# A planned matmul-tanh-multiply kernel: fewer split multiplications on VectorE, and the general path's transfers on GpSimd's queue

## The chip, the core and the metric

One core of a Trainium2 chip. The metric is the device time of one execution in microseconds (us), the median of the runs of a kernel; less is better. Engines are named as in the profile: PE is TensorE, DVE is VectorE, ACT is ScalarE, POOL is GpSimd, SP is SyncE. A "q" behind an engine (SPq, POOLq) is its instruction sequencer, which issues DMAs and handles waits.

## The reference, cut

```python
x  : (16, 512, 1024) float32      # 8192 rows of 1024
w1 : (1024, 768), w2 : (1024, 768) float32
y1 = matmul(x, w1); y2 = matmul(x, w2)
return tanh(y1) * y2              # (16, 512, 768) float32
```

Two matrix products with the same left side, and one element-wise combination of both.

## The kernel before, in words

**Tiling.** The 8192 rows are 64 row tiles of 128 (`mt` 0 to 63). The 768 columns of an output are cut in a first 512 (`F`) and a last 256 (`G`). The weights lie in SBUF as float16 in three column blocks of 512: `a` is w1's first 512, `b` is w2's first 512, `g` holds w1's last 256 beside w2's last 256. The inner dimension of 1024 is cut in two halves of four 128-deep slices (`KH` = 4).

**Head and triples.** The first four row tiles (`HEAD`) are computed plainly (lines 419 to 434) while the weights still arrive. The other 60 are taken in 20 triples (i = 0 to 19) of three row tiles. Three row tiles by two halves by three column blocks would be 18 block products; each triple gets by with 15 (`p0` to `p14`, line 441), by sums of left blocks (`A_SUMS`, operations `S...`, line 410, on DVE) and of weight blocks (`B_SUMS`, once for all triples), and by sums of results (`C_OPS`). A product is four matmuls of 128x128 by 128x512 that accumulate in one PSUM bank. Eight banks rotate.

**What happens to the results.** `C_OPS` lists the operations of a triple behind the products, and what each needs:
- `copyN`, `seedN` (line 446, ACT): copy a bank to SBUF (`arena`), or into another bank on which a later product goes on accumulating (`seed16` before `p2`; `seed56` before `p8`).
- `addN` (line 449, DVE): the sum of a bank and a copy, back into a bank or into SBUF. `p9` waits for `add312`, `p12` for `add64`, `p4` for `add60`, `p3` and `p2` for `add52` and `seed16`, and `p14` overwrites what `seed56` reads.
- `t0`, `t1`, `t2` (line 455, ACT): tanh of 512 columns into the output tile `o`; `th0` to `th2` the same for the last 256.
- `m0`, `m1`, `m2` (line 459, `c_mul`, DVE): multiply the tanh in `o` with the 512 columns of y2 in a bank, in place; `mh0` to `mh2` the same for the last 256. With this the bank is free for a later product, and the row tile can be stored (line 416, SP's queue).

A name with a number behind a dot is that operation in that triple: `m1.10` is `m1` of triple 10. Products of the next triple are mixed in (`PE_ORDER`, line 69): `p4.10` runs between products of triple 11.

**Where a multiplication is split.** Lines 704 to 711 enter the multiplications. For `m0`, `m1`, `m2` of every triple but the last they make two operations of 256 columns (`m0x` and `m0y`), each with a cost of 0.335 for the planner; for the last triple one of 512 columns at 0.6.

**What sets the order.** The class `Planner` (lines 75 to 223) plays the whole kernel through at build time from these costs, due times and needs: at each step it takes the operation that can start soonest, by due time among those that tie, and gives each accumulation chain one of the eight banks. The products' order on PE is fixed (`plan.strict`, line 502); that of DVE, ACT and of the queues comes from the planner, and is then kept in the program (`pin`). So a cost that is entered differently can change the order of neighbouring operations and the numbers of the banks.

**The flag and the general path.** The fast way holds for inputs whose absolute sums lie in certain limits. ACT sums them on the way (lines 379 to 387), DVE and PE make one flag of them near the end (`f1` to `f5`), and all five engines read it (line 766) and branch (line 767). If the flag is set, `general_path` (line 771) computes everything again in a plain loop. For the inputs used here the flag is zero and its body is not executed; a short block for the other side of the branch evens out the semaphores.

Of the kernel before, what the change touches and what calls it, by code (L numbers as in the profile page):

```python
# [226 lines left out]
def kernel(  # L227
# [7 lines left out]
    nc = tc.nc  # L235
# [9 lines left out]
    TRIPLES = (MT - HEAD) // 3  # L245
# [4 lines left out]
    WARM = 512, 512, 512, 512, 512, 512, 512  # L250
    FILL = 512, 512, 256
    AHEAD, FREE = 4, 3
    S_AHEAD = 4.0
    LATER = {mt: 66.0 + 13.0 * mt for mt in range(HEAD - 1)}
    bf16, f16, f32, i32 = mybir.dt.bfloat16, mybir.dt.float16, mybir.dt.float32, mybir.dt.int32

    xf = x.flatten_outer_dims().rearrange("(mt p) k -> mt p k", p=P)
    of = out.flatten_outer_dims().rearrange("(mt p) n -> mt p n", p=P)
    wr = [w.rearrange("(ko ki) n -> ki ko n", ki=P) for w in (w1, w2)]
# [403 lines left out]
    def needed(i, v):  # L663
        return min([slot_of[i, o[0]] for o in C_OPS if o[1] == "p" and o[4] == v] + [needed(i, u) - 0.5 for u, a, b, _ in A_SUMS if v in (a, b)])

    for i in range(TRIPLES):
        for name, kind, needs, *_ in C_OPS:
            soonest[i, name] = max([until[i, n] for n in needs] + ([slot_of[i, name]] if kind == "p" else []))
            until[i, name] = soonest[i, name] + TIME[kind] + 0.2
        for v, a, b, how in A_SUMS:  # L670
            op(f"S{v}.{i}", {"dve": 0.335}, None, x_needs(i, a) + x_needs(i, b), x_sum, i, v, a, b, how,
               hold=needed(i, v) - S_AHEAD if i > 1 else 0.0,
               behind=[f"{r}.{i - S_BUFS}" for r in a_readers[v]] if i >= S_BUFS else first_done)
            for u in (a, b):
                if not u & (u - 1):
                    xt_readers[HEAD + 3 * i + (u.bit_length() - 1) // 2].append(f"S{v}.{i}")
        for o in C_OPS:
            name, kind, needs = o[:3]
            needs = [f"{n}.{i}" for n in needs]
            chains = sorted({(i, p) for p in o[3:6] if isinstance(p, str) and p[0] == "c"})  # L680
            if kind == "p":
                needs += x_needs(i, o[4]) + w_needs(o[5])
                op(f"{name}.{i}", {"pe": SLOT}, slot_of[i, name], needs, product, i, *o[3:], chains=chains,
                   behind=[f"m{HEAD - 1}y0{KO - 1}"] if (name, i) == ("p3", TRIPLES - 1) else [])
                if not o[4] & (o[4] - 1):
                    xt_readers[HEAD + 3 * i + (o[4].bit_length() - 1) // 2].append(f"{name}.{i}")
                continue
            if kind in ("seed", "copy", "add"):
                before = []
                if o[3][0] == "s":  # L690
                    before = [f"{r}.{i - C_BUFS}" for r in readers[o[3]]] if i >= C_BUFS else all_casts
                if kind == "add":
                    op(f"{name}.{i}", {"dve": 0.6}, None, needs, c_add, i, *o[3:], behind=before, chains=chains, seeds=True)
                else:
                    op(f"{name}.{i}", {"act": 0.495}, None, needs, c_copy, i, *o[3:], behind=before, chains=chains, seeds=True)
                continue
            r = o[3]
            mt = HEAD + 3 * i + r
            due = soonest[i, name] + LAST
            if kind in ("t", "th"):  # L700
                lo, n = (0, F) if kind == "t" else (F, G)
                op(f"{name}.{i}", {"act": 0.5 if n == F else 0.285}, due, needs, c_tanh, i, r, o[4], lo, n, o[5],
                   behind=reuse_out(mt) + ([f"{FIRST_READER[name]}.{i}"] if i == TRIPLES - 1 and name in FIRST_READER else []), chains=chains)
            elif kind == "m" and i < TRIPLES - 1:
                for t in range(2):
                    op(f"{name}{'xy'[t]}.{i}", {"dve": 0.335}, due + 1, needs, c_mul, i, r, o[4], t * G, G, t * G, chains=chains)
                    outs[mt].append(f"{name}{'xy'[t]}.{i}")
            else:
                lo, n, at = (0, F, 0) if kind == "m" else (F, G, G)
                op(f"{name}.{i}", {"dve": 0.6 if n == F else 0.335}, due + 1, needs, c_mul, i, r, o[4], lo, n, at, chains=chains)  # L710
                outs[mt].insert(0 if kind == "m" else 1, f"{name}.{i}")
    for mt in range(MT):
        i = (mt - HEAD) // 3 if mt >= HEAD else -1
# [23 lines left out]
    for mt in range(HEAD, MT):  # L737
        i, r = divmod(mt - HEAD, 3)
# [16 lines left out]
    for n in sorted(soon, key=lambda n: plan.start_of[n]):  # L755
        o = plan.ops[n]
# [3 lines left out]
    for n in order:  # L760
        if n not in soon:
            o = plan.ops[n]
# [8 lines left out]
def general_path(tc, xf, wr, of, N, F):  # L771
    nc = tc.nc
    P = 128
    MT, _, K = xf.shape
    KO = K // P
    G = N - F
    f16, f32, i32 = mybir.dt.float16, mybir.dt.float32, mybir.dt.int32
    with ExitStack() as stack:
        pool = lambda name, bufs, **k: stack.enter_context(tc.tile_pool(name=name, bufs=bufs, **k))
        once = pool("general", 1)  # L780
        work = pool("general_work", 2)
        ps = pool("general_ps", 2, space=bass.MemoryType.PSUM)

        def powers(total, n, tag):
            p = work.tile([P, n], f32, name=tag)
            nc.vector.tensor_scalar(p.bitcast(i32), total.bitcast(i32), 0x7F800000, None, ALU.bitwise_and)
            nc.vector.tensor_scalar(p, p, 2.0 ** -100, 2.0 ** 100, ALU.max, ALU.min)
            r = work.tile([P, n], f32, name=tag + "r")
            nc.vector.reciprocal(r, p)
            return p, r  # L790

        ones = once.tile([P, P], f32, name="g_ones")
        nc.vector.memset(ones, 2.0 ** -12)
        asum = once.tile([P, 2, KO], f32, name="g_asum")
        junk = once.tile([P, K], f16, name="g_junk")
        wf = [once.tile([P, KO, N], f32, name=f"g_wf{t}") for t in range(2)]
        wh = [once.tile([P, KO, N], f16, name=f"g_wh{t}") for t in range(2)]
        w_p = once.tile([P, 2], f32, name="g_wp")
        for t in range(2):
            nc.sync.dma_start(wf[t], wr[t])  # L800
            for k in range(KO):
                nc.scalar.activation(junk[:, :N], wf[t][:, k, :], ACT.Abs, accum_out=asum[:, t, k:k + 1])
            part = work.tile([P, 1], f32, name="g_part")
            nc.vector.tensor_reduce(part, asum[:, t, :], mybir.AxisListType.X, ALU.add)
            total = ps.tile([P, F], f32, name="g_total")
            nc.tensor.matmul(total[:, :1], ones, part, start=True, stop=True)
            p, r = powers(total[:, :1], 1, "g_w")
            nc.vector.tensor_copy(w_p[:, t:t + 1], p)
            for k in range(KO):
                nc.vector.tensor_scalar(wh[t][:, k, :], wf[t][:, k, :], r, None, ALU.mult)  # L810

        with tc.For_i(0, MT, 1) as i:
            xt32 = work.tile([P, K], f32, name="g_x")
            nc.sync.dma_start(xt32, xf[i])
            s = work.tile([P, 1], f32, name="g_s")
            nc.scalar.activation(junk, xt32, ACT.Abs, scale=2.0 ** -12, accum_out=s)
            p, r = powers(s, 1, "g_xp")
            xh = work.tile([P, K], f16, name="g_xh")
            nc.vector.tensor_scalar(xh, xt32, r, None, ALU.mult)
            xt = work.tile([P, KO, P], f16, name="g_xt")  # L820
            nc.sync.dma_start_transpose(xt, xh)
            scale = work.tile([P, 2], f32, name="g_scale")
            nc.vector.tensor_scalar(scale, w_p, p, None, ALU.mult)
            o = work.tile([P, N], f32, name="g_o")
            for lo, n in ((0, F), (F, G)):
                y = [ps.tile([P, F], f32, name=f"g_y{t}") for t in range(2)]
                for t in range(2):
                    for k in range(KO):
                        nc.tensor.matmul(y[t][:, :n], xt[:, k, :], wh[t][:, k, lo:lo + n],
                                         start=k == 0, stop=k == KO - 1)  # L830
                nc.scalar.activation(o[:, lo:lo + n], y[0][:, :n], ACT.Tanh, scale=scale[:, :1])
                nc.vector.scalar_tensor_tensor(o[:, lo:lo + n], y[1][:, :n], scale[:, 1:2], o[:, lo:lo + n],
                                               ALU.mult, ALU.mult)
            nc.sync.dma_start(of[i], o)


# [28 lines left out]
```

## Time and profile before

| | |
|---|---|
| median of 3 runs (lowest, highest) | 298.52 us (298.41, 298.60) |
| the profiled execution | 298.88 us |
| its span, first to last instruction | 297.1 us, so 1.8 us lie around it |
| PE busy | 290.1 us (98%), granted clock 0.998 |
| DVE busy | 259.7 us (87%), 597 instructions |
| ACT busy | 226.3 us (76%) |
| POOL busy | 50.4 us (17%) |

The profile is one execution. A row of the groups of instructions gives line, engine, operation, what is written from what, the count, then busy time and the mean of one, then the engine's idle time ahead of them and what ended it. A row of the timeline gives the start and the length in us, and stands for several instructions where it ends with x2 or more. Records of one engine overlap a little, since an instruction's last part lies beside the next one's first: the distance from start to start is what one costs its engine. On PE a 512-column matmul is recorded with 379 ns, and in a full stretch one starts every 0.216 us.

### The profile page before, as it was taken

The numbers are of one execution on the slowest core, as the hardware profiler recorded it, in microseconds if no ns is written. First come the engines' busy times: TensorE is split into PE (matmuls) and PEld (weight loads), VectorE is DVE, ScalarE is ACT, GpSimd is POOL, SyncE is SP. The second block draws the span as 40 slices with busy tenths as digits, with TensorE's granted clock in tenths as the row PEclk, the third lists the DMA queues.
The fourth block names the chain that finished last, engine by engine and source line by source line (L and its number), as shares of the span: only waits on it lengthen the run. The fifth ranks groups of instructions, "written<-read, shape, count | busy, mean of one in ns | idle before, by whom it ended". The sixth has DMA issues, their size and how long they took to land. (4 is left out here: it accounts for less than half of the span.)

```text
span 297.1 us, 4747 instructions
## 1 busy us (share of the span) xinstructions
PE 290.1 (98%) x1374; PEld 132.4 (45%) x1374; DVE 259.7 (87%) x597; ACT 226.3 (76%) x453; POOL 50.4 (17%) x129
## 2 busy tenths in 40 slices
PE   8999999999999999999999999999999999999993
PEld 3445444444444444444444444444444444444441
DVE  1679899989999998989989899898989989898884
ACT  2596898799978979798797988768677776868441
POOL 0073133132221111213111111202021110000000
PEclk9999999999999999999999999999999999999999
DMA  6999999999999999999999999999999999041234
GB/s 230 387 300 207 182 157 147 189 202 260 197 251 250 225 294 274 162 177 286 221 204 192 285 240 206 282 158 308 151 269 198 279 253 282 18 162 53 107 143 161
DMA packets 84428, 63.51 MB, mean 214 GB/s; under 512 B 62768, under 2 KB 66608, under 8 KB 84400
## 3 DMA queue, kind: packets, MB, share of 16 engines
q1 hardware_dynamic: 73600, 44.84, 63.7%
q0 software_dynamic: 9792, 16.78, 34.9%
q10 hardware_dynamic: 1008, 1.57, 1.5%
q8 instruction: 11, 0.18, 0.3%
q14 instruction: 17, 0.14, 0.2%
HBM read 39.85 MB, written 25.17 MB: 219 GB/s over the span
## 5 line engine op out<-in xcount | busy, mean ns | idle before, releaser
L443 PE MATMUL bank<-b,early_x 128*128 128x512 f16 x640 | 148.4, 379 | 0.1
L443 PEld LDWEIGHTS <-early_x 128*128 128x128 f16 x800 | 78.0, 98 | 94.7 <-DVE early_x L411 0.6
L453 DVE TENSOR_TENSOR bank<-bank,arena 128x512 f32<-128x512 f32 x100 | 69.6, 697 | 13.1 <-ACT arena L447 8.9
L447 ACT ACTIVATE arena<-bank 128x512 f32<-128x512 f32 x100 | 59.3, 596 | 28.5 <-PE bank L443 28.3
L461 DVE TENSOR_TENSOR o<-o,bank 128x256 f32<-128x256 f32 (+1 forms) x177 | 68.1, 420 | 6.5 <-ACT o L456 5.7
L380 ACT ACTIVATE junk<-xh 128x1024 f16<-128x1024 f16 x60 | 63.4, 1056 | 0.2
L443 PEld LDWEIGHTS <-xT 128*128 128x128 f16 x400 | 39.0, 98 | 47.5 <-issue 1.3
L443 PE MATMUL bank<-b,xT 128*128 128x512 f16 x240 | 58.3, 379 | 0.0
L456 ACT ACTIVATE o<-bank 128x256 f32<-128x256 f32 (+1 forms) x80 | 34.4, 436 | 16.1 <-DVE bank L453 12.8
L443 PE MATMUL bank<-wh,xT 128*128 128x512 f16 x160 | 41.1, 379 | 0.4 <-DVE bank L453 0.4
L443 PE MATMUL bank<-wh,early_x 128*128 128x512 f16 x160 | 40.9, 379 | 0.0
L352 POOL DMA_DIRECT2D xh<-in_x_dram x60 | 31.7, 529 | 35.8 <-ACT o L456 20.2
L480 POOL CAST held<-xT 128x1 f32<-128x1 f16 x54 | 13.6, 252 | 137.8 <-DMA xT<-xh 137.7
L411 DVE TENSOR_TENSOR early_x<-early_x,xT 128x512 f16<-128x512 f16 x80 | 33.3, 419 | 0.5
L447 ACT ACTIVATE bank<-bank 128x512 f32<-128x512 f32 x40 | 21.6, 578 | 8.8 <-DVE bank L453 7.7
L456 ACT ACTIVATE o<-arena 128x512 f32<-128x512 f32 x40 | 25.2, 629 | 0.6 <-DVE arena L453 0.5
L420 PE MATMUL bank<-wh,xT 128*128 128x512 f16 x72 | 18.5, 379 | 0.4 <-DVE wh L358 0.3
L411 DVE TENSOR_TENSOR early_x<-xT,xT 128x512 f16<-128x512 f16 x40 | 16.8, 420 | 0.0
L411 DVE TENSOR_TENSOR early_x<-xT,early_x 128x512 f16<-128x512 f16 x40 | 16.8, 419 | 0.0
L453 DVE TENSOR_TENSOR bank<-arena,bank 128x512 f32<-128x512 f32 x20 | 13.9, 695 | 1.5
L453 DVE TENSOR_TENSOR arena<-arena,bank 128x512 f32<-128x512 f32 x20 | 13.6, 682 | 0.0
L453 DVE TENSOR_TENSOR arena<-bank,arena 128x512 f32<-128x512 f32 x20 | 13.6, 681 | 0.0
(47 smaller groups left out, 136.3 us busy)
## 6 DMA issues: line engine op xcount, KB each, us to landing
out_dram<-o SPq DMA_DIRECT2D x60, 384.0 KB, 5.5
xh<-in_x_dram POOLq DMA_DIRECT2D x60, 256.0 KB, 6.4
arena<-in_w_dram SPq DMA_DIRECT2D x12, 256.0 KB, 5.4
early_x<-in_x_dram SPq DMA_DIRECT2D x8, 256.0 KB, 5.0
arena<-in_w_dram ACTq DMA_DIRECT2D x4, 256.0 KB, 5.8
wh<-in_w_dram POOLq DMA_DIRECT2D x8, 128.0 KB, 5.2
xT<-xh SPq DMA_TRANSPOSE x57, 6.6
out_dram<-o SPq DMA_DIRECT2D x4, 128.0 KB, 2.4
```

The source lines that it names most:

```text
L352: pin(nc.gpsimd.dma_start(xh(mt), xf[mt]))
L380: pin(nc.scalar.activation(junk[:, :src.shape[-1]], src, ACT.Abs, scale=scale, accum_out=sums[:, column:column + 1]))
L411: pin(engine[e].tensor_tensor(x_operand(i, v), x_operand(i, a), x_operand(i, b), OP[how]))
L420: pin(nc.tensor.matmul(bank(chain)[:, :rhs.shape[-1]], xt(mt)[:, k, :], rhs, start=first, stop=k == KO - 1, skip_group_check=True))
L443: pin(nc.tensor.matmul(place(i, dst), x_operand(i, a)[:, k, :], w_rhs(b, k), start=begins and k == 0, stop=k == KH - 1, skip_group_check=T ...
L447: pin(nc.scalar.activation(place(i, dst), place(i, src), ACT.Copy, scale=float(sign)))
L453: pin(nc.vector.tensor_tensor(place(i, dst), a, b, ALU.add if signs == (1, 1) else ALU.subtract))
L456: pin(nc.scalar.activation(out_tile(HEAD + 3 * i + r)[:, lo:lo + n], place(i, src)[:, :n], ACT.Tanh, scale=float(sign)))
L461: pin(nc.vector.tensor_tensor(o, o, place(i, src)[:, at:at + n], ALU.mult))
L480: pin(nc.gpsimd.tensor_copy(held, xt(mt)[:, 0, :1]))
```

## The change

Two edits. A new constant `HALVED = 4` takes the place of `TRIPLES - 1` in the condition that splits a multiplication: `m0`, `m1`, `m2` are now split in triples 0 to 3 alone, and are one operation of 512 columns in triples 4 to 19 (before, in triple 19). And in `general_path` the loads of the weights and of the row tiles, and the store of the result, are issued from GpSimd's queue instead of SyncE's; its transpose stays on SyncE.

```diff
-    S_AHEAD = 4.0
+    S_AHEAD, HALVED = 4.0, 4
...
-            elif kind == "m" and i < TRIPLES - 1:
+            elif kind == "m" and i < HALVED:
                 for t in range(2):
                     op(f"{name}{'xy'[t]}.{i}", {"dve": 0.335}, due + 1, needs, c_mul, i, r, o[4], t * G, G, t * G, chains=chains)
...
         for t in range(2):
-            nc.sync.dma_start(wf[t], wr[t])
+            nc.gpsimd.dma_start(wf[t], wr[t])
...
             xt32 = work.tile([P, K], f32, name="g_x")
-            nc.sync.dma_start(xt32, xf[i])
+            nc.gpsimd.dma_start(xt32, xf[i])
...
-            nc.sync.dma_start(of[i], o)
+            nc.gpsimd.dma_start(of[i], o)
```

## The prediction

> **What bounds the kernel now.** I asked first whether PE ever waits where the change acts, which is from triple 4 on, from about 88 us. The busy times of all engines in that stretch (columns: length, then busy us and instructions of PE, PEld, DVE, ACT, POOL, granted clock, DMA share, GB/s):
>
> ```profile
> 85.00:270.00 185.00, 185.00 (x859) 83.86 (x858) 168.42 (x387) 148.51 (x300) 28.41 (x76) 1.00 1.07 221
> ```
>
> PE is busy for 185.00 of 185.00 us at the full clock, and 185 us by 859 matmuls is 0.215 us each, the same as their distance from start to start. So this is not slow matmuls under a full label: PE is at its rate. The waits of PE over the whole run, in full:
>
> ```profile
> PE bank L330 <- DVE ones L752: 1.1, 1, 1.1
> PE bank L443 <- DVE bank L453: 0.4, 1, 0.4
> PE bank L420 <- DVE wh L358: 0.3, 1, 0.3
> PE bank L370 <- DMA early_x<-in_x_dram: 0.3, 1, 0.3
> ```
>
> Three of the four lie in the first 14 us. The one at line 443 is at 51.86 us, in the triples that stay split. DVE is busy for 91% of the stretch and still makes PE wait for nothing, so DVE time saved there is no kernel time in itself.
>
> **Part 1, the whole multiplications.** 15 triples (4 to 18) by 3 lose a pair of halves and gain one whole: 90 instructions out, 45 in. Their rows, by shape:
>
> ```profile
> L461 DVE TENSOR_TENSOR o<-o,bank 128x256 f32<-128x256 f32 x174 | 66.2, 415 | 5.6 <-ACT o L456 5.1
> ...
> L461 DVE TENSOR_TENSOR o<-o,bank 128x512 f32<-128x512 f32 x3 | 2.1, 685 | 0.9 <-ACT o L456 0.7 <-issue 0.2
> ```
>
> The means alone give 2 x 415 - 685 = 145 ns a pair, but records overlap. What a half costs DVE is its distance to the next, and the timeline of DVE in triple 10 shows it:
>
> ```profile
> 171.69 0.41 DVE L461 TENSOR_TENSOR o<-o,bank 128x256 f32<-128x256 f32 x1
> 172.18 0.70 DVE L453 TENSOR_TENSOR bank<-bank,arena 128x512 f32<-128x512 f32 x1
> 172.79 1.07 DVE L461 TENSOR_TENSOR o<-o,bank 128x256 f32<-128x256 f32 x3
> 173.78 0.68 DVE L453 TENSOR_TENSOR arena<-arena,bank 128x512 f32<-128x512 f32 x1
> 174.38 0.42 DVE L411 TENSOR_TENSOR early_x<-xT,xT 128x512 f16<-128x512 f16 x1
> 174.84 0.70 DVE L453 TENSOR_TENSOR bank<-bank,arena 128x512 f32<-128x512 f32 x1
> 175.45 0.68 DVE L453 TENSOR_TENSOR arena<-bank,arena 128x512 f32<-128x512 f32 x1
> ```
>
> Three halves from 172.79 to 173.78 are 0.33 us each; a 512-column operation takes 0.60 (173.78 to 174.38). A pair costs 0.66 and a whole 0.60: 0.06 x 45 = 2.7 us of DVE time, 0.18 of each triple's 12.95, all of it beside a full PE. As PE has no gap there to give back, I count 0.
>
> Can it cost? A whole one can't be interrupted for 0.60 instead of 0.33 us, so what is urgent behind it comes up to 0.27 later, and the planner reorders around it. The built program's order shows what moves: SP's and POOL's queues keep theirs; on DVE, `add8` goes ahead of `add52` in triples 4, 7 and 10; on ACT, at the same places, `seed16` goes behind `t1` and the next triple's `seed56`; bank numbers are renamed. With triple 10's rows in the new order: `m0.10` from 171.69 to a next start at 172.29, `add312.11` there (0.11 later), `m2.10` 172.89, `add64.11` 173.49 (0.29 earlier), `add8.10` 174.55 (behind the copy that ends at 174.51), `add52.10` 175.15, ending 175.85. On ACT, `t1.10` at 175.27, `seed56.11` 175.77, `seed16.10` 176.27 to 176.85. Who waits for that:
>
> ```profile
> 175.57 1.07 ACT L447 ACTIVATE bank<-bank 128x512 f32<-128x512 f32 x2 [0.45 <-DVE bank L453]
> ```
>
> ```profile
> 177.16 1.03 PE L443 MATMUL bank<-wh,early_x 128*128 128x512 f16 x4
> 178.03 1.24 PE L443 MATMUL bank<-b,xT 128*128 128x512 f16 x5
> ```
>
> The two seeds end at 176.16 and 176.65. `p14.11` (177.16) has 0.51 to spare behind `seed56` now, and 0.81 in the new order (end 176.35); `p3.10` (178.03) has 1.87 behind `seed16` now and 1.18 then. `p9` starts 1.42 us or more behind `add312` in triples 4 to 18, so 0.11 to 0.2 more is covered.
>
> The shortest cover is that of the multiplication itself: `p7` two triples on takes the bank that `m1` frees.
>
> ```profile
> 180.14 1.08 DVE L461 TENSOR_TENSOR o<-o,bank 128x256 f32<-128x256 f32 x3
> ...
> 181.48 0.81 PE L443 MATMUL bank<-wh,xT 128*128 128x512 f16 x3
> ```
>
> The row at 180.14 is `mh1.10`, `m1x.10`, `m1y.10`; the last ends at 181.22, 0.27 ahead of PE, and so it is, within 0.02, in ten of the 13 triples from 4 to 16 (0.60 in the others). One whole multiplication from 180.47 ends at 181.16: 0.06 earlier, not later. `p3.18` at 280.79 has 0.26 behind `seed16.18`, whose order stays.
>
> **The last triple** has no cover left, and small things count. PE's gaps there are 0.06 us at 285.27, 0.06 at 286.63 and 0.14 at 289.70, 0.26 in all (a 256-column matmul starts 0.109 before the next):
>
> ```profile
> 285.27 1.02 PE L443 MATMUL bank<-b,early_x 128*128 128x512 f16 x4
> ...
> 289.70 1.89 PE L443 MATMUL bank<-b,xT 128*128 128x512 f16 x8
> ```
>
> In the built order the filler matmuls of line 420 that stood before `p5.19` and `p4.19` move behind `p14.19`, and `add60.19` goes ahead of `mh0.18`. `m1.18` spares 0.06, so `add2.19` ends at 285.16 and `p5.19` starts at 285.21 (0.11 idle behind `p0.19`). `th0.18` at 284.44 and `copy56.19` at 284.73 let `add60.19` run 285.36 to 286.06, `p4.19` 286.11. Two more products of 0.86 and eight fillers of 0.109 bring `p3.19` to 289.57; the chain behind `p4` (3.07 us from 286.63 to 289.70 now) would allow 289.18. So `p3.19` starts 0.13 earlier, and what follows it is unchanged: -0.13 us. The bounds here are -0.54 (all 0.26 of gaps, and the 0.28 by which DVE's last multiplication waits for its engine behind the last matmul) and +0.27 (one blocking that nothing covers). I take -0.13.
>
> **Part 2, GpSimd's queue.** `general_path` doesn't run, so its transfers cost nothing by either queue. What does run is the other side of the branch, which evens semaphores: SP has one bump instead of five, POOL two waits and one software-queue bump. POOL reads the flag at 275.5 and then idles to the final barrier at 296.3, 20 us of cover. The same kind of bump took 0.03 us at the start; the dearest POOL row, the L352 transfers, is 0.53 each. SP's four bumps fewer are 0.3 us, but SP then waits for the last store to land:
>
> ```profile
> SPq L860 <- DMA out_dram<-o: 0.2, 1, 0.2
> ```
>
> The wait only grows. With the cover gone on either side, it would be 0.3 less, or 0.5 more (SP's time from its branch, 294.7, to its first wait behind it, 295.2, in the trace); I count 0, since both covers are long.
>
> **The sum.** 298.88 - 0.13 = 298.75 for the profiled execution, which lies 0.36 over the median; so 298.4 for the median.
>
> **The rivals.**
> - **PE starts to wait for whole multiplications** (slower). The place is `p7` behind `m1`. It decides from 0.27 us: a whole `m1` that starts more than 0.32 later than `m1x` does now makes PE wait (0.27, and the 0.06 by which it ends sooner). For it speaks that DVE is 91% busy and that its order is fixed in advance; against it that nothing ahead of `m1` changes and that it ends 0.06 sooner. If a 0.60 block too many stood ahead in those ten triples, (0.60 - 0.33) x 10 = 2.7, 301.1 us; in three of them, the reordered ones, 0.8, 299.2. Chance 0.08. The Trainium skill (Perfetto Trace Analysis, Optimizing Scalar/DVE Operations) has the rule that speaks against this change: where VectorE isn't saturated but causes bubbles elsewhere, smaller instructions let work finish sooner. By that rule undoing the split would bring bubbles; the trace has no bubble in 85 to 270 us for the split to have healed, so it doesn't bear the rule out here.
> - **The tail gives all it has** (faster): -0.54, 298.0; still within 0.2%. A gain above that would need PE to run faster than 0.216 us a matmul, or the wait at 51.86 us to go, and the order is the same up to there. Chance of that 0.04.
> - **The branch side costs**: +0.5, 298.9, if POOL or SP became last; against it the 20 us. Within 0.2% too.
> - That only the multiplications change anything (the general path's edit does nothing here) is part of the forecast.
>
> **How the numbers follow.** About 0.2% (0.6 us) is what a measurement of this kernel can tell from no change. No change that can be told: 0.87, with the branch side and the full tail in it. Slower by PE's waits: 0.08, and 0.01 for what I don't see: 0.09. Faster: 0.04. The range is 298.0 (the whole tail) to 298.9 (a branch cost, or one uncovered block with the median's own spread), and leaves out under 0.2.
>
> **What would show it.** PE busy for the whole of 85 to 270 again; 84 halves and 48 wholes at line 461; DVE's busy share lower with PE's the same; `p3.19` at 289.6; SP's wait for the last store longer than 0.2. PE waits on line 461 or 453 between 88 and 270 us would prove me wrong.

## The result, and the profile after

The changed kernel takes 298.24 us, the median of 22 runs (297.88 to 298.70). 22 runs of the kernel before beside it have a median of 298.70 us, so the three runs known beforehand were some 0.2 us low. The ratio is 0.9982 [0.9975, 0.9989]: about 0.5 us less, just under the bound of 0.2%. The forecast was 0.13 us. The profiled execution took 298.26 us with a span of 296.7 (before: 298.88 and 297.1).

From triple 4 on PE has no gap, as before, and DVE is busy for 2.2 us less. The busy times from 85 to 270 us of the kernel after (columns as before):

```profile
85.00:270.00 185.00, 185.00 (x859) 83.87 (x857) 166.20 (x346) 148.20 (x300) 28.51 (x76) 1.00 1.11 220
```

The waits of PE over its whole run, in full. None lies behind 52 us:

```profile
PE bank L330 <- DVE ones L752: 1.3, 1, 1.3
PE bank L370 <- DMA early_x<-in_x_dram: 0.4, 1, 0.4
PE bank L443 <- DVE bank L453: 0.3, 1, 0.3
PE bank L420 <- ACT xT L356: 0.2, 1, 0.2
```

The multiplications by shape (count, then busy us and mean ns of one), 84 halves and 48 wholes:

```profile
L461 DVE TENSOR_TENSOR o<-o,bank 128x256 f32<-128x256 f32 x84 | 33.5, 418 | 5.6 <-ACT o L456 5.2
L461 DVE TENSOR_TENSOR o<-o,bank 128x512 f32<-128x512 f32 x48 | 31.8, 681 | 0.6 <-ACT o L456 0.3 <-DMA out_dram<-o 0.2
```

Triple 10 on DVE; the kernel runs 0.10 later here, because it starts 0.23 later in its span and has not made up all of that:

```profile
171.79 0.68 DVE L461 TENSOR_TENSOR o<-o,bank 128x512 f32<-128x512 f32 x1
172.39 0.69 DVE L453 TENSOR_TENSOR bank<-bank,arena 128x512 f32<-128x512 f32 x1
172.99 0.68 DVE L461 TENSOR_TENSOR o<-o,bank 128x512 f32<-128x512 f32 x1
173.58 0.68 DVE L453 TENSOR_TENSOR arena<-arena,bank 128x512 f32<-128x512 f32 x1
174.18 0.42 DVE L411 TENSOR_TENSOR early_x<-xT,xT 128x512 f16<-128x512 f16 x1
174.64 0.69 DVE L453 TENSOR_TENSOR arena<-bank,arena 128x512 f32<-128x512 f32 x1
175.25 0.69 DVE L453 TENSOR_TENSOR bank<-bank,arena 128x512 f32<-128x512 f32 x1
```

`m0.10`, `add312.11`, `m2.10` and `add64.11` follow each other at 0.60, and `add8.10` (174.64) now stands ahead of `add52.10` (175.25), as the built order said. ACT and PE behind them:

```profile
175.90 1.06 ACT L447 ACTIVATE bank<-bank 128x512 f32<-128x512 f32 x2
```

```profile
177.26 1.03 PE L443 MATMUL bank<-wh,early_x 128*128 128x512 f16 x4
178.13 0.59 PE L443 MATMUL bank<-b,xT 128*128 128x512 f16 x2
```

In the first row `seed56.11` ends at 176.48 and `seed16.10` at 176.96, so `p14.11` (177.26) has 0.78 to spare and `p3.10` (178.13) has 1.17.

The last triple on PE:

```profile
284.34 1.03 PE L443 MATMUL bank<-b,xT 128*128 128x512 f16 x4
285.31 1.94 PE L443 MATMUL bank<-b,early_x 128*128 128x512 f16 x8
287.09 1.89 PE L443 MATMUL bank<-wh,early_x 128*128 128x512 f16 x8
288.82 1.04 PE L420 MATMUL bank<-wh,xT_kept 128*128 128x256 f16 x8
289.69 1.89 PE L443 MATMUL bank<-b,xT 128*128 128x512 f16 x8
```

From `p0.19` (284.34) to `p3.19` (289.69) it takes 5.35 us; before, 5.46 (284.24 to 289.70). This is the 0.11 us that the change gains on PE. In the profile it only cancels the 0.10 that the head was late: the last store is issued at 293.38 us in both. Yet the span ends 0.38 us sooner. **What the two executions differ by lies behind the last store.** There the sequencer of SP waits for the stores, and the landing of the last one is faster. The first fence of each pair is of before, the second of after; first the page's row of instruction packets (packets, MB, share), then the last store alone (count, size, us from issue to landing), then SP's wait for stores at line 860 (us, times, longest):

```profile
q14 instruction: 17, 0.14, 0.2%
```

```profile
q14 instruction: 16, 0.13, 0.1%
```

```profile
out_dram<-o SPq DMA_DIRECT2D x1, 128.0 KB, 2.6
```

```profile
out_dram<-o SPq DMA_DIRECT2D x1, 128.0 KB, 2.3
```

```profile
SPq L860 <- DMA out_dram<-o: 0.7, 2, 0.4
```

(Before: 0.2.) The trace has the single events. A store is done when 16 increments of its semaphore are there, each sent by a packet of 4 bytes. Before, 15 of the last store's arrive from 295.41 to 295.58 us, and the sixteenth at 296.02. After, all arrive from 295.41 to 295.64. Before, the last of these 4-byte packets begins at 295.359 us, and 6 ns later an 8 KB instruction packet of 309 ns. The trace does not say which DMA engine moves a packet; that both are on one engine is read from these 6 ns. And before, DVE's jump over the code of `general_path` to the kernel's last block takes 0.57 us (branch at 293.49, first instruction behind it at 294.06); after, 0.21. The 309 ns packet and the long jump are present in one kernel and absent from the other. The packet begins 1.87 us behind the branch. DVE is already past the jump then, by 1.30 us, so it does not wait for this packet.

**Theory.** The end is the later of two things, and about 1.06 us of barrier behind it: (1) SP's own way, which is longer by its semaphore bumps; and (2) the landing of the last store, which is late when DVE's jump sets off a fetch of code. The whole multiplications shorten DVE's stream, and the jump's target becomes its 795th instruction instead of the 843rd. Instruction packets have 8 KB here, and DVE's come some 128 instructions apart; by the places at which DVE's other packets are fetched, one such block ends at about the 839th, an estimate (the runs below put it between the 829th and the 843rd). The jump then crosses no such end, no fetch meets the store, and (2) comes 0.37 sooner. Part 2 takes four bumps from SP, and (1) gets shorter. Either alone leaves the other. **Rivals:** the gain comes from DVE's saved 2.7 us; or from the queue alone; or it is scatter. The theory took this form only behind the first four runs. "Theory T" in their expectations had SP's bumps alone as the source of what is gained behind the last store; the part with the fetch ("theory F") came with the fifth.

### The profile page after: what moved, and what is told of

Same layout as the page of the kernel before. It is cut to its first block, busy times and chain, and to the rows that moved or that the text cites. A ratio compares the mean times of both kernels' runs of the same rounds, so it can differ in the third digit from the quotient of the medians.

```text
span 296.7 us, 4680 instructions
## 1 busy us (share of the span) xinstructions
PE 289.9 (98%) x1374; PEld 132.3 (45%) x1374; DVE 257.4 (87%) x552; ACT 225.9 (76%) x453; POOL 49.9 (17%) x129
## 5 line engine op out<-in xcount | busy, mean ns | idle before, releaser
L461 DVE TENSOR_TENSOR o<-o,bank 128x256 f32<-128x256 f32 (+1 forms) x132 | 64.4, 513 | 6.1 <-ACT o L456 5.5
L480 POOL CAST held<-xT 128x1 f32<-128x1 f16 x54 | 13.0, 241 | 152.4 <-DMA xT<-xh 152.4
```

What stands on the lines that cost most here:

```text
L461: pin(nc.vector.tensor_tensor(o, o, place(i, src)[:, at:at + n], ALU.mult))
L480: pin(nc.gpsimd.tensor_copy(held, xt(mt)[:, 0, :1]))
```

## The experiments

Ratios are against the kernel before on the same chip, "store to SP" is the time from the issue of the last store until SP has passed its wait for it, from the trace.

**Part 1 alone.** The diff's three `nc.gpsimd` lines are put back to `nc.sync`.

> Part 1 alone: whole multiplications in triples 4 to 19, the general path's transfers left on SP. Theory T (the gain has two sources: 0.1 us of PE gaps in the last triple, and about 0.35 us in SP's way to the end, where five semaphore bumps and the wait for a store's landing stand ahead of the final waits): the time falls by the PE part alone, 0.1 us (ratio 0.9997), p3 of the last triple starts 0.1 earlier against p0 of that triple, and SP reaches its final block at about 295.2 us as before. Rival R1 (the whole gain comes from the multiplications, the later landing of the last store in the profile of before was chance): ratio 0.998.

298.38 us, ratio 0.9987 [0.9973, 1.0001]. The jump takes 0.21 us and the store lands after 2.2:

```profile
out_dram<-o SPq DMA_DIRECT2D x1, 128.0 KB, 2.2
```

SP has no wait for it at line 860 at all, and passes 2.42 us after the issue: its own way is last. That is 0.22 less than before's 2.64. Theory T, which had only 0.1 us for this kernel, missed that: part 1 moves the landing too.

**Part 2 alone.** The kernel before, with

```diff
-            nc.sync.dma_start(wf[t], wr[t])
+            nc.gpsimd.dma_start(wf[t], wr[t])
```

and likewise the other two.

> Part 2 alone: the general path's loads and store on GpSimd, multiplications as before. Theory T: SP bumps one semaphore instead of five, reaches its final block 0.8 us earlier (294.5 instead of 295.2), and the time falls by 0.2 to 0.4 us (ratio 0.9987 to 0.9993). Rival R1: no change (ratio 1.000). My prediction on record had no change here, since SP waits for the last store to land anyway.

298.70 us, ratio 1.0001 [0.9991, 1.0012]. SP comes to its wait sooner and waits longer, for a landing that is as late as before:

```profile
SPq L860 <- DMA out_dram<-o: 1.0, 2, 0.7
```

Store to SP 2.63 us: the prediction's step on part 2, alone, was right, and the 0.2 to 0.4 us less that theory T expected did not come.

**The queue of ACT instead.** As the last, with `nc.scalar`; SP keeps its five bumps.

> The general path's loads and store on ACT's queue instead of SP's, multiplications as before. They stay hardware-generated transfers, and the built program shows the same five bumps on SP. Theory T (the bumps on SP count, not the queue that would issue the transfers): no change, ratio 1.000. Rival R2 (it is the length of SP's code in the general path, or what SP's queue would issue, that delays SP's jump to the end): as with GpSimd's queue, 0.2 to 0.4 us less.

298.71 us, 1.0002 [0.9993, 1.001]; 17 packets, jump 0.57, SP's wait 0.2, store to SP 2.62: as before in each.

**More bumps on SP.** The weight loads of `general_path` are cut in three and two pieces, so that SP evens eight semaphores.

```diff
-            nc.sync.dma_start(wf[t], wr[t])
+            for ks in ((slice(0, 2), slice(2, 4), slice(4, KO)), (slice(0, 4), slice(4, KO)))[t]:
+                nc.sync.dma_start(wf[t][:, ks], wr[t][:, ks])
```

> The opposite dose: the general path's weight loads cut in five pieces on SP, so that eight bumps stand on SP's way to the end, the one of the last store's semaphore among them; multiplications as before. Theory T: SP can leave the bumps only when the last store has landed (about 295.7 to 296.0 us), then jumps (0.5) and runs through twelve final waits (0.06 each): 0.9 us longer, ratio 1.003. Rival R1 (the end is set by the last landing alone, whatever SP does): ratio 1.000.

300.13 us, 1.005 [1.0034, 1.0066], so 1.5 us more. Three more bumps cost far more than three of the others, because a bump waits for its semaphore's own stores:

```profile
SPq L767 <- SPq L767: 2.1, 4, 0.8
```

Before, this row was 0.6 with one wait, for an earlier store. Now one of the bumped semaphores is the last store's own, and SP takes up its way to the end only behind that landing: store to SP 3.94. Theory T had the direction, and 0.9 us. The side of the branch that runs can be the critical path; my range for it had 0.5 us.

**Shorter code that isn't executed.** The kernel before; the general path's 16 scalings are two.

```diff
-            for k in range(KO):
-                nc.vector.tensor_scalar(wh[t][:, k, :], wf[t][:, k, :], r, None, ALU.mult)
+            nc.vector.tensor_scalar(wh[t], wf[t], r, None, ALU.mult)
```

> The kernel before, with only the code of the general path made shorter for DVE: sixteen scalings of one weight slice each become two of all eight slices. That path isn't executed, so every executed instruction but the length of the jump over it stays. Theory F (what part 1 gained beyond PE's 0.11 us is code loading at the end: in the kernels with halves DVE's jump to the final block, from its 769th instruction to its 843rd, leaves a block of 128 instructions, an 8 KB code packet follows on one DMA engine, and the last store's sixteenth completion there comes 0.35 us or more after the fifteenth): with the target at the 829th, DVE needs 0.21 instead of 0.57 us from its jump to the next instruction, the straggler is gone, and the time falls by 0.3 us (ratio 0.999). Rival R1 (the gain is that of the stores that leave earlier in the last triple): no change.

The target is now DVE's 829th instruction. 298.61 us, 1.0007 [0.9993, 1.002]: the time expected didn't show. The profile expected did: 16 packets, jump 0.21, all increments within 0.15 us, landing after 2.2. But SP's way is then last at 2.43, which leaves 0.2 us, and that lies at the edge of the interval.

**Longer code that isn't executed.** The changed kernel; each of those scalings is cut in six of 128 columns.

```diff
             for k in range(KO):
-                nc.vector.tensor_scalar(wh[t][:, k, :], wf[t][:, k, :], r, None, ALU.mult)
+                for c in range(0, N, 128):
+                    nc.vector.tensor_scalar(wh[t][:, k, c:c + 128], wf[t][:, k, c:c + 128], r, None, ALU.mult)
```

> The changed kernel (both parts), with only the code of the general path made longer for DVE: each of the sixteen scalings cut in six, so that the jump goes from the 721st instruction to the 875th instead of the 795th. Theory F: the jump takes 0.57 us again, the straggler of the last store is back, and the time is 0.3 us longer than the changed kernel's 298.24, near the kernel before (ratio 0.9995 to 1.000 to before). Rival R1: stays at 0.9982.

The target is the 875th instruction. 298.49 us, 0.9997 [0.9987, 1.0007]. Jump 0.57, the sixteenth increment 0.36 behind the fifteenth, store to SP 2.62. Most of the gain is gone, though every instruction executed is the changed kernel's.

**One more operation ahead of `m1`**, in triples 4 to 18 of the changed kernel: a multiplication of 128x224 on a tile that nothing else uses, 0.302 us from start to start.

```diff
+        if r == 1 and n == F and 4 <= i <= 18:
+            pin(nc.vector.tensor_tensor(pad, pad, pad, ALU.mult))
```

> The changed kernel with one more DVE operation of 224 columns (0.30 us by 224 of 256 columns of the 0.33 row) ahead of m1 in triples 4 to 18; its result is used by nobody. The step under test is the cover of p7 behind m1: 0.33 us in the profile of the changed kernel in eleven of these triples, 0.6 or more in the others. If it holds, PE still waits for nothing between 85 and 270 us, and the time is that of the changed kernel, within 0.2 us. If the cover is smaller than I read it, PE waits about eleven times.

298.61 us, 1.0006 [0.9989, 1.0024]: 0.1 us over the kernel before on its chip, where the changed kernel lies 0.3 to 0.5 under it, so some 0.5 us over the changed kernel. `p7` never waits in the profile, as a cover of 0.33 leaves room for 0.302. What DVE's lateness costs there comes elsewhere, at `p14` of one triple, behind ACT's seed:

```profile
PE bank L444 <- ACT bank L448: 1.0, 1, 1.0
```

This execution took 299.65 us, 1.0 over the median, so most of the others can't have had this wait in full.

**Two of them.**

> The same with two such operations, 0.6 us. If the cover is 0.33, PE waits 0.27 in each of eleven triples: 2.9 us more than the changed kernel, about 301.1 us, the ratio to before 1.008. A rival (what bounds is DVE's total load, then 96% of a triple): no wait at p7, less than 0.5 us.

301.39 us, 1.0091 [1.0072, 1.0109]: 3.2 to 3.3 us over the changed kernel, by the distance of each to the kernel before on its chip. That is near the 2.9 expected, but not by the expected way. The pair costs 0.73 us and not 0.60, since the second operation starts 0.42 behind the first, whose result it reads; with 0.73 the same sum would give 0.40 in each of eleven triples, 4.4 us. The stretch from 85 to 270 us, and PE's waits:

```profile
85.00:270.00 185.00, 184.47 (x851) 83.14 (x850) 171.36 (x370) 146.23 (x297) 28.29 (x75) 1.00 1.06 218
```

```profile
PE bank L444 <- DVE bank L454: 0.9, 2, 0.7
PE bank L478 <- DVE count L475: 0.6, 1, 0.6
PE bank L444 <- DVE o L465: 0.3, 1, 0.3
```

PE is "busy" for 184.47 of 185 us, yet starts 851 matmuls where it started 859. By starts, seven gaps of 0.04 to 0.41 us add up to 1.55: `p7` waits in two triples, `p14` in five. Behind that come 0.80 at the flag's matmul (line 474 of the kernel before) and 0.83 in the last triple. Once PE has waited it runs later against DVE, and the next triples have cover again. So a rival's price "in each of ten triples" was not what happens; it is paid a few times, and at the end.

**Both mended without touching a multiplication.** The kernel before, with part 2 and with the short code.

> The kernel before with all its halves, with the three transfers on GpSimd's queue and with the general path's sixteen scalings written as two. Theory (the end is the later of SP's own way and the landing of the last store, and the late landing comes with the instruction packet that DVE's jump to the end fetches): the fetch goes and SP's way is short, so both are mended and the end comes 0.37 us sooner with no multiplication changed: ratio 0.9988, DVE's jump 0.21 us, the last store passed 2.27 us after its issue, SP's wait for it 0.4 or more. Rival (the gain behind the last store comes from the whole multiplications, which end DVE's work sooner): nothing, 1.000.

298.48 us, 0.9995 [0.9986, 1.0004], 0.14 us less than before. The time can't tell the two apart: it leaves room for the 0.9988 expected and for nothing. The profile does: 16 packets, jump 0.21, no late increment, store to SP 2.30, and SP waits for a store that lands after 2.3:

```profile
out_dram<-o SPq DMA_DIRECT2D x1, 128.0 KB, 2.3
```

```profile
SPq L859 <- PEq L859: 0.7, 2, 0.5
SPq L859 <- DMA out_dram<-o: 0.7, 2, 0.4
```

From the last store's issue to the end of the span it is 3.36 us, against 3.71 before. With all halves in place and PE's gaps in the last triple as before, the end behind the store is the changed kernel's.

**The changed kernel again,** on the chip of the last.

> The changed kernel once more, beside the others on one chip. Every theory expects what it showed: ratio 0.9980 to 0.9986. It is the measure for the other three.

298.29 us, 0.9990 [0.9981, 0.9999]: 0.3 us less here, where the first 22 runs gave 0.5. Tail on PE as in the first profile, store to SP 2.30, 16 packets.

**The longer code again,** beside it.

> The changed kernel with each of the general path's scalings cut in six, once more, now beside the changed kernel itself. No instruction that runs differs from the changed kernel's. Theory: the jump fetches again (0.57 us) and the last store lands late, so 0.35 us more than the changed kernel: ratio about 0.9995. Rival (the length of code that isn't executed can't matter): the changed kernel's 0.9983.

298.55 us, 0.9992 [0.9977, 1.0007], 0.26 over the changed kernel. 17 packets, jump 0.57, the sixteenth increment 0.38 late, store to SP 2.58:

```profile
q14 instruction: 17, 0.14, 0.2%
```

```profile
out_dram<-o SPq DMA_DIRECT2D x1, 128.0 KB, 2.6
```

The last store was issued at 293.25 in this one and at 293.28 in the changed kernel; the spans are 296.9 and 296.6.

**No multiplication split.**

```diff
-    S_AHEAD, HALVED = 4.0, 4
+    S_AHEAD, HALVED = 4.0, 0
```

> The changed kernel with HALVED = 0: the multiplications of the first four triples are whole too. Theory (PE waits for no multiplication, whole or half; the end behind the last store is the changed kernel's): as the changed kernel, 0.998 to 0.9986, with the wait of line 443 in the early triples at 0.2 to 0.6 us as in all profiles. Rival (in the first triples, where DVE also converts weights, a whole one comes too late for PE): 0.3 to 0.6 us more, 0.9993 to 1.0003, with PE waits between 40 and 85 us.

298.95 us, 1.0016 [1.0001, 1.0031]: 0.66 more than the changed kernel, above what either expected. The profiled execution took 299.51 us, 0.56 over the median, so it shows more than the median has. In it PE's gaps from 36 to 66 us add up to 0.76 (0.22 at 38.86, 0.09 at 47.59, 0.45 at 52.36). The same stretch has 0.40 in the changed kernel's second profile, 0.63 in its first and 0.73 before, nearly all of it the wait at about 52 us and a gap at about 66. Only the first two gaps, 0.31 together, are in none of the others. The rest is at the end, where the last two stores' sixteenth increments come over 1 us late (store to SP 3.25):

```profile
SPq L860 <- DMA out_dram<-o: 1.5, 1, 1.5
```

DVE's jump takes 0.21 and there are 16 packets. Yet the trace has an 8 KB packet of 309 ns that begins at 295.25 us, amid the packets of the last two stores, and a second one, of 744 ns, at 295.53; the last increments of these stores are sent at 295.55 and 296.22, the other 30 by 295.48. And the step from DVE's load of the flag to its first branch is 0.43 us instead of 0.08, longer by 0.35, as the long jump is. So here, too, a fetch seems to meet the stores, from another place in DVE's code, where the jump's length doesn't show it. That the two packets cost a whole microsecond was not tried by itself.

No version tried was shown to be faster than the changed kernel.

The ends in one table. "Late" is the sixteenth increment of the last store behind the fifteenth:

| kernel | DVE's jump, us | q14 packets | late, us | store to SP, us | what SP passes last |
|---|---|---|---|---|---|
| before | 0.57 | 17 | 0.44 | 2.64 | landing |
| part 2 alone | 0.57 | 17 | 0.34 | 2.63 | landing |
| ACT's queue | 0.57 | 17 | 0.41 | 2.62 | landing |
| long code, twice | 0.57 | 17 | 0.36, 0.38 | 2.62, 2.58 | landing |
| more bumps on SP | 0.57 | 17 | 0.43 | 3.94 | own way |
| part 1 alone | 0.21 | 16 | none | 2.42 | own way |
| short code alone | 0.21 | 16 | none | 2.43 | own way |
| short code and part 2 | 0.21 | 16 | none | 2.30 | landing |
| after, twice | 0.21 | 16 | none | 2.27, 2.30 | landing |
| none split | 0.21 | 16 | 1.03 | 3.25 | landing |

In the six profiles with the long jump the 309 ns packet begins 1.87 to 1.89 us behind the branch, 1.30 to 1.32 behind DVE's next instruction, and 5 or 6 ns behind the last store's last 4-byte packet.

## Why the prediction was right, and where it was not

**PE is not bound by DVE in the middle: right.** 185.00 of 185.00 again, with 859 matmuls, and DVE's 2.2 us less gave nothing there.

**The moved operations: right.** `p14.11` 0.78 to spare (forecast 0.81), `p3.10` 1.17 (1.18), `p7` 0.33 or more behind `m1` (0.33), no wait.

**The tail: right.** The 0.11 idle behind `p0.19` is there (0.10), and `p3.19` comes 0.11 earlier instead of 0.13.

**Part 2 at nothing: right alone, wrong beside part 1.** The step said that SP's four bumps fewer are 0.3 us and that "SP then waits for the last store to land", so "the wait only grows". That holds as long as the landing is late, as part 2 alone shows (wait 0.7, ratio 1.0001). I took the landing as fixed. Part 1 moves it 0.37 sooner, and then SP's own way decides: 2.42 with the bumps, 2.27 to 2.30 without. So part 2 is worth 0.12 to 0.15 us on top of part 1. Two of the step's prices were too low as well. SP leaves the bumps 0.77 us sooner behind the last store's issue and not 0.3, since one of the four that go had waited for an earlier store to land. And POOL's software-queue bump takes 1.55 us and not 0.03; it starts at 276.37 us, and POOL's idle time covers it.

**The term that was missing: the jump's code.** I counted what runs, and not where it stands. The change shifts DVE's last block against the boundaries of its instruction fetch, that fetch goes, and with it the late increment. By the profiles the terms are 0.11 (PE's tail), 0.22 (part 1 behind the store) and 0.12 to 0.15 (part 2 there), together 0.45 to 0.48, against 0.46 measured between the medians (298.70 and 298.24) and 0.33 in the second comparison. Of the 0.13 forecast, 0.11 came as forecast; the larger part of the gain lies where the prediction counted 0. The Trainium skill (Runtime: NRT & Kernel Launch, Instruction fetch mechanics) states that a taken branch to a page outside the current window forces a DMA fetch before execution goes on; I had left that rule out of the prediction. The trace agrees that the jump is dearer, 0.57 against 0.21 us, and that a packet follows it; but DVE goes on 1.30 us before that packet begins, so a stall until it has arrived is not what the 0.57 shows. What the 0.36 us more are spent on is not settled. The section gives blocks of 16 KiB; here only PE's packets have that size, and those of the other engines have 8 KB. That a fetch delays a store is not in that section; the runs show the two together.

How sure that is: the jump, the packet and the late increment come and go together in 11 of the table's 12 profiles, all but that with none split, and short and long unexecuted code switch them without a change in what runs. The times bear out one half of it. The two timings of the longer code lie 0.02 and 0.07 us under the kernel before, those of the changed kernel 0.46 and 0.33 under it; no single pair of intervals separates them, but both differences have the expected sign and nearly the size. The other half doesn't show in the times: the two kernels with short code and all halves lie 0.10 over and 0.14 under the kernel before, where the ends of their profiles would give 0.21 and 0.35 less. So it stays open whether the whole multiplications do more for the median than the 0.11 us seen in PE's tail. That the packet's position on one engine is what delays the increment is read from times that coincide; it wasn't tried by itself.

**The median.** 298.4 lies 0.16 over the result, and so near it partly by luck: it rests on a base of 298.52 from three runs, and on 298.70 the same sum gives 298.57, 0.33 over. The result lies in the range because the lower bound of 298.0 allowed 0.54 us of gains in the last triple; 0.11 of them came, and the rest of the gain lies elsewhere.

**The rivals.** PE's waits for whole multiplications didn't come; one more operation of 0.302 us in each triple is nearly borne, two of 0.73 together are not. The full tail didn't come. The branch side moved, to the other side: it gave instead of costing.

## What to carry to other kernels

Where several things must be over for a kernel to end, price a change of each with the other as it will be after the change: by the ends of the profiles, two that are worth 0.2 and 0 alone were worth 0.37 together. On a result of a few tenths of a microsecond, look at what follows the last store, and at where the code lies, before crediting the edit that was meant. And count starts, not busy time, when asking whether PE waits: a matmul's record of 379 ns over a distance of 216 hides gaps of up to 0.16 us.

## What the runs showed of the hardware that was not expected

- Unexecuted code can cost time: with 80 more instructions in a branch not taken, DVE's jump took 0.57 us instead of 0.21, one more instruction packet came, and the last store landed 0.3 us later.
- The last store, of 128 KB, takes 2.2 to 2.3 us to land, and 2.6 in the six profiles in which an instruction packet of 8 KB (309 ns) begins 5 or 6 ns behind its last 4-byte packet.
- POOL's software-queue bump on the side of the branch that runs takes 1.55 us here, where the one at the start of the kernel takes 0.03.
- A semaphore bump on SP can cost more than its own length: with eight of them, one had to wait for the last store, and the kernel took 1.5 us longer. With five, one waits some 0.5 us for an earlier store.
- A second profile of one kernel moves by its head: PE's gap at about 52 us, by starts, is 0.60 before, 0.50 after, and 0.10 to 0.60 over all profiles. This scatter is larger than the tail's gain, so the stages were compared by distances within a profile.
- In all nine profiles that have part 2 the first transfer is issued at 0.98 us in the span, in the five without it at 0.74 or 0.75. 1.54 to 1.69 us lie around the span with part 2, and 1.77 to 2.00 without. For the two kernels compared the two differences cancel (0.23 and 0.24), which is why a span alone doesn't give the gain; why the second is smaller is not settled.
